# A hybrid decoder block in split fp32: norms of the mixers ended by GpSimd, an earlier weight load and gelu table, square adds on VectorE, and a later start of the second matrix's left factors

## The chip, the cores and the metric

The kernel runs on one core of one Trainium2 chip. The metric is the device time of one execution in microseconds (us), which is the core's span and about 1.7 us around it. The engines are called by the profile's names: PE (TensorE, matrix multiplication), DVE (VectorE), ACT (ScalarE), POOL (GpSimd) and SP (SyncE, which issues most loads).

## The reference

One decoder block over 2048 positions of 1024 features in fp32:

```
h = rms_norm(x, norm1_g)
proj = h @ w_in                                   # u_a, v_a, val_b, gate_b: 512 columns each
# mixer A, four heads of 128 channels
u = gelu(u_a);  v = layer_norm(gelu(v_a), sgu_ln_g, sgu_ln_b)
a = u * (tril(sgu_w[head]) @ v + sgu_b[head])     # over the positions within chunks of 128
# mixer B, four groups of 128 channels
g = val_b * sigmoid(gate_b)
c = depthwise_conv1d(g, conv_w, causal, width 31) + conv_b
c = silu(layer_norm(c, per group of 128 channels))
x = x + concat([a, c]) @ w_out
x = x + relu(rms_norm(x, norm2_g) @ w_ff1)**2 @ w_ff2      # 1024 -> 4096 -> 1024
return rms_norm(x, final_g)
```

## The kernel before

**Arithmetic.** Every fp32 operand of a large product is split into a high part, which a cast on ACT rounds, and a low part, which is the difference, made mostly by POOL (`w_lo`, `h_lo`, `fo_lo`, `w1o`, `w2p`) and now and then by DVE. A product is three matmuls of 128x512 (high x high, low x high, high x low; `mm3`).

**Stages.** The 2048 positions are four blocks of 512. For each block `stage_v` makes the 512 columns of `v_a` (tile `pvv`, four weight tiles of 512 KB, each two slices of 128 features), applies gelu (`gv`) and takes mean and variance on DVE (`vmv`), and then makes `u` (`pu`, gelu at L582). Between them stands the normalisation of `gv` at L585, after which `gate` multiplies it with the masked matrix `wt` (`sgu`). `stage_g` makes gate and value columns (`pg`, `pv`) and starts the convolution: 31 taps on DVE, run in the background (`conv_chain`, `acc<-g,vec,acc`). A finished convolution goes through `conv_tail`: transpose on PE (`ct`), statistics on DVE (`mv`), normalise on ACT (L304, `c<-ct,nb,rs`), transpose back (`cb`), silu (L313, `part<-cb,vec`). `stage_o` is the output projection (`po`).

**A norm's end.** Both norms (`centre` for `gv`, `conv_tail` for `c`) need a scale `rs` = (variance + eps)^-0.5 and a bias `nb` = -mean x rs, 4 values for each partition. DVE makes `ve` = variance + eps, POOL raises it to the power -0.5, DVE multiplies -mean by the result, and ACT normalises with both. In `conv_tail` each `yield` puts the rest off until the clock that the program keeps for PE or DVE has reached the time given.

**The start.** The first four weight tiles come through `load_w`, in order, on SP's queue. `norm1` is a generator whose first step loads two tiles `xin` of the input for the row norm; behind it SP issues `wt` and `cbias`. ACT applies a gelu for the first time at L549.

**The MLP** multiplies matrices in 2x2 blocks with seven products in place of eight (`ORDER`). Its left factors are sums of weight quarters, split in two parts (`w1o`, `w2p`), made during other work and sent to device memory (`w_d`). Its right factors are sums of activations (`fraw`, split into `fo_hi` and `fo_lo`). `down_chunk(pair, n, after)` does step n of the second matrix for a pair of blocks: 28 groups of six matmuls into `py`, each added by DVE to the residual (`x<-py,x`). Between groups `beside` lets other generators run; how many left factors of the second matrix it makes is set by `pace["w2"]`, an amount added at each call. In the last step of a pair (n == 7) every finished `x` is squared on ACT and added up (`square_add`), eight for each block, and a sum over features on PE (`ssum`) gives the final norm.

**What sets the order.** Inside `tc.manual_schedule()` (the output projection, the first matrix, the last step) instructions run in the order in which the code issues them. Everywhere else, the mixers and 15 of the 16 `down_chunk`s among it, a scheduler with a timeline of its own orders each engine's instructions, so an edit in one place also shifts others near it. Each engine then runs its own list in order.

Of the kernel before, what the change touches and what calls it, by code (L numbers as in the profile page):

```python
# [12 lines left out]
AF = mybir.ActivationFunctionType  # L13
ALU = mybir.AluOpType

P = 128
# [20 lines left out]
LAG = 3.0  # L37
# [45 lines left out]
def hybrid_block_kernel(  # L83
# [68 lines left out]
    def tiny(name, n=4):  # L152
        return small.tile([P, n], F32, tag=f"{name}{n}", name=name)
# [83 lines left out]
    nc.vector.memset(ones, 1.0)  # L237
    nhalf = const.tile([P, 1], F32, name="nhalf")
    nc.vector.memset(nhalf, -0.5)
    idle = t2.tile([P, 1024], BF16, tag="tmp", name="idle")[:, :512]  # L240
    nc.vector.memset(idle, 1.0)
    first_bank = tp_tile("first")
# [13 lines left out]

    def centre(mv, rs):

        rsqrt(rs, mv[:, :, 1], 1.0)
        nb = tiny("nb")  # L260
        dve.scalar_tensor_tensor(nb, mv[:, :, 0], -1.0, rs, op0=ALU.mult, op1=ALU.mult)
        return nb


# [18 lines left out]
    def conv_tail(j, c, dst):  # L283

        pt = tp_tile("ct")
        st = small.tile([P, 4, 6], F32, tag="st", name="st")
        mv = small.tile([P, 4, 2], F32, tag="mv", name="mv")
        rs, ve = tiny("rs"), tiny("ve")
        for i in range(4):
            pe4.transpose(pt[:, i * P:(i + 1) * P], c[:, i * P:(i + 1) * P], ident)  # L290
        yield pe.time + 1.0
        for i in range(4):
            dve.bn_stats(st[:, i, :], pt[:, i * P:(i + 1) * P])
        for i in range(4):
            dve.bn_aggr(mv[:, i, :], st[:, i, :])
        dve.tensor_scalar(ve, mv[:, :, 1], 1.0, EPS, op0=ALU.mult, op1=ALU.add)
        yield dve.time + LAG
        gps.tensor_tensor(rs, ve, nhalf.to_broadcast([P, 4]), op=ALU.pow)
        yield pe.time + 1.0
        nb = tiny("nb")  # L300
        dve.scalar_tensor_tensor(nb, mv[:, :, 0], -1.0, rs, op0=ALU.mult, op1=ALU.mult)
        yield dve.time + LAG
        for i in range(4):
            nc.scalar.activation(  # L304
                c[:, i * P:(i + 1) * P], pt[:, i * P:(i + 1) * P], AF.Identity,
                scale=rs[:, i:i + 1], bias=nb[:, i:i + 1])
        yield pe.time + LAG
        pb = tp_tile("cb")
        for i in range(4):
            pe4.transpose(pb[:, i * P:(i + 1) * P], c[:, i * P:(i + 1) * P], ident)  # L310
        yield pe.time + 1.0
        y = dst.place(4 + j, "y")
        nc.scalar.activation(y, pb, AF.Silu, scale=v(V_CG, j), bias=v(V_CBE, j))  # L313
        dst.done(4 + j)
        yield None
# [160 lines left out]
            load_resid(b, kp)  # L476
            yield

    def square_add(acc, src, last=False):

        sq = tmp("sq")[:, :src.shape[1]]
        nc.scalar.activation(sq, src, AF.Square)
        if not acc or last:
            acc.append(sq)
        else:
            gps.tensor_tensor(acc[0], acc[0], sq, op=ALU.add)

    def feature_sums(acc, n, pc=None):

# [197 lines left out]
        nc.sync.dma_start(xk[kp], xt[0, kp].rearrange("p a t -> p (a t)"))  # L687
    r0 = tiny("r1")
    stats = norm1(0, r0)
    next(stats)  # L690
    nc.sync.dma_start(wt, sgu_wt.rearrange("h s t -> s h t"))
    nc.sync.dma_start(cbias, sgu_b.unsqueeze(0).to_broadcast([P, 4, P]))
# [546 lines left out]
    def down_chunk(pair, n, after):  # L1239
# [4 lines left out]
        for i, j in STEPS:  # L1244
# [17 lines left out]
            if n == 7 and LAST[a, t] == i:  # L1262
                done[t] += 1
                if final:
                    sq = tmp("sq")
                    nc.scalar.activation(sq, x, AF.Square)
                    acc = accs[t]
                    if not acc or done[t] > (7 if t else 6):
                        acc.append(sq)
                    else:  # L1270
                        later(1, lambda acc=acc, sq=sq: gps.tensor_tensor(
                            acc[0], acc[0], sq, op=ALU.add))
                    if t == 0 and k_of(done[0]):
                        gained(dn["x"][2], k_of(done[0]))
                else:
                    square_add(accs[t], x)
                if done[t] == 8:
                    if not final:
                        queue.append(finish(2 * pair + t, accs[t]))
                    elif t:  # L1280
                        queue.append(finish_third(3, accs[t]))
                    else:
                        while due:
                            put_off()
                        while queue:
                            if next(queue[0], 0) == 0:
                                queue.pop(0)
                        ends.append(finish_last(2, accs[t], w2[4][0][:, 0, :P], ops[4][0][:, :512]))
# [29 lines left out]
        while due:  # L1318
            beat()
    reopen_banks(mid, "d", mm=8)  # L1320
    pace["w2"] = W2_PACE[3]

    def after_down(pair):
        def after(n, i):
            next(gens, 0)
            if pair == 0 and 2 <= n < 5 and i == 6:
                next(gens)
            if n == 7 and pair == 0:
                for k in range(8):
                    if k * 7 // 8 == DOWN.index(i):  # L1330
                        load_x1(2 + k % 2, k // 2)
        return after
# [57 lines left out]
```

## Time and profile before

| | us |
|---|---|
| median of three runs | 1831.97 (1828.97 to 1837.33) |
| the profiled execution | 1831.89 |
| its span | 1830.2 |
| mean granted clock of PE | 0.997 |
| PE busy | 1809.3 |
| DVE busy | 1330.8 |
| POOL busy | 1233.3 |
| ACT busy | 758.6 |

The busy times are sums over the whole span. The list of waits gives for each pair of waiting and releasing line the total, the number of times and the longest; a row of a timeline gives the start, the time taken, the engine, the line in the code, `out<-in` by the program's names and, in brackets, how long the engine was idle before and what ended that. Lines are those of the kernel before. The three mixers' blocks without output projection run up to about 330 us, the first matrix from about 450 us, and the second from about 1265 us.

### The profile page before, as it was taken

What the parts mean: (1) busy time and instruction counts of PE and PEld (TensorE: products, weight loads), DVE (VectorE), ACT (ScalarE), POOL (GpSimd) and SP (SyncE); (2) the same over time, 40 slices, a digit from 0 to 9 for tenths busy, and PEclk for the clock granted to TensorE, in tenths of its full rate; (3) what the DMA queues carried; (4) which work ended last, traced back from release to release, by engine and by line L of the source; (5) the groups of instructions that cost most, each with busy time, mean ns of one, the idle gap of its engine ahead of it and who ended that gap; (6) DMA issues with size and microseconds to landing.
All of it is one profiled execution on the core that took longest, in us unless ns stands there. A gap on an engine that the chain in (4) does not pass through costs nothing. (4 is left out here: it accounts for less than half of the span.)

```text
span 1830.2 us, 23249 instructions
## 1 busy us (share of the span) xinstructions
PE 1809.3 (99%) x8080; PEld 1488.5 (81%) x8080; DVE 1330.8 (73%) x1825; ACT 758.6 (41%) x1172; POOL 1233.3 (67%) x775
## 2 busy tenths in 40 slices
PE   9999999999999999999999999999999999999998
PEld 6888878888888888888888888888788888888886
DVE  5699997997998985632567787676866568665655
ACT  6345565454445445455354545432322231212112
POOL 4575975883766666699878989776945465444434
PEclk9999999999999999999999999999999999999999
DMA  8342655432645456685557778998987679767652
GB/s 327 112 164 91 229 178 213 184 125 83 220 150 189 161 195 202 215 293 204 208 184 266 270 258 298 355 408 335 412 326 248 252 272 327 299 238 256 254 191 93
DMA packets 131686, 424.74 MB, mean 232 GB/s; under 512 B 14576, under 2 KB 15216, under 8 KB 131568
## 3 DMA queue, kind: packets, MB, share of 16 engines
q1 hardware_dynamic: 96000, 329.12, 50.5%
q10 hardware_dynamic: 35568, 94.13, 13.2%
q8 instruction: 64, 1.05, 0.2%
q14 instruction: 54, 0.44, 0.1%
HBM read 302.60 MB, written 120.59 MB: 231 GB/s over the span
## 5 line engine op out<-in xcount | busy, mean ns | idle before, releaser
L78 PE MATMUL py<-fo_hi,w2o 128*128 128x512 f32 x1792 | 555.9, 391 | 0.8 <-DVE x L78 0.8
L78 POOL TENSOR_TENSOR fo_lo<-fraw,fo_hi 128x1024 fp32r<-128x1024 f32 x111 | 274.4, 2481 | 252.9 <-ACT fo_hi L160 210.7
L78 DVE TENSOR_TENSOR x<-py,x 128x512 f32<-128x512 f32 x448 | 300.9, 687 | 185.8 <-PE py L78 185.4
L78 PEld LDWEIGHTS py<-fo_hi,w2o 128*128 128x128 f32 x1792 | 337.1, 188 | 72.0 <-DVE x L78 1.2
L78 PE MATMUL py<-hop,w1o 128*128 128x512 f32 x1536 | 363.8, 390 | 0.5 <-ACT c L982 0.4
L78 PE MATMUL py<-fo_lo,w2o 128*128 128x512 f32 x896 | 349.7, 390 | 0.9 <-POOL fo_lo L78 0.8
L78 PEld LDWEIGHTS py<-hop,w1o 128*128 128x128 f32 x1536 | 287.6, 188 | 62.4 <-issue 1.4
L78 DVE SCALAR_TENSOR_TENSOR acc<-g,vec,acc 128x512 f32<-128x512 f32 x464 | 322.9, 746 | 1.2
L160 ACT CAST fo_hi<-fraw 128x1024 fp32r<-128x1024 f32 x112 | 117.0, 1052 | 413.7 <-PE py L78 218.0
L78 POOL TENSOR_TENSOR w_lo<-raw,w_hi 128x1024 fp32r<-128x1024 f32 (+1 forms) x94 | 224.1, 2392 | 53.9 <-ACT w_hi L160 39.6
L78 POOL TENSOR_TENSOR w1o<-wraw,w1o 128x512 fp32r<-128x512 f32 x120 | 172.0, 1438 | 55.6 <-ACT w1o L810 43.4
L78 PEld LDWEIGHTS py<-fo_lo,w2o 128*128 128x128 f32 x896 | 168.6, 188 | 37.9 <-POOL fo_lo L78 2.6
L78 PE MATMUL pz<-hop,w1o 128*128 128x512 f32 x768 | 183.8, 390 | 0.0
L78 POOL TENSOR_TENSOR w1o<-ws,w1o 128x512 fp32r<-128x512 f32 x90 | 128.7, 1433 | 66.4 <-ACT w1o L810 62.6
L78 PEld LDWEIGHTS pz<-hop,w1o 128*128 128x128 f32 x768 | 143.8, 188 | 29.8
L78 DVE TENSOR_TENSOR fraw<-fraw 128x1024 f32<-128x1024 f32 x64 | 93.1, 1455 | 13.3 <-POOL fo_lo L78 13.2
L993 ACT ACTIVATE c<-c 128x512 f32<-128x512 f32 x128 | 80.8, 631 | 52.5 <-DVE c L78 52.0
L78 PE MATMUL po<-m_hi,w_hi 128*128 128x512 f32 x256 | 101.1, 395 | 0.0
L78 PE MATMUL po<-m_hi,w_lo 128*128 128x512 f32 x256 | 99.8, 390 | 0.6 <-POOL w_lo L78 0.6
L78 PE MATMUL po<-m_lo,w_hi 128*128 128x512 f32 x256 | 99.7, 389 | 0.0
L78 DVE TENSOR_TENSOR px<-px,c 128x512 f32<-128x512 f32 x32 | 22.3, 698 | 100.9 <-PE px L78 67.8
L78 POOL TENSOR_TENSOR w2p<-wraw,w2p 128x512 fp32r<-128x512 f32 x64 | 93.5, 1463 | 2.6 <-ACT w2p L810 2.6
(155 smaller groups left out, 2947.9 us busy)
## 6 DMA issues: line engine op xcount, KB each, us to landing
w2o<-w_d SPq DMA_DIRECT2D x224, 512.0 KB, 6.0
w_d<-w2p ACTq DMA_DIRECT2D x112, 512.0 KB, 5.4
wraw<-in_w SPq DMA_DIRECT2D x92, 512.0 KB, 4.7
f_d<-c ACTq DMA_DIRECT2D x128, 256.0 KB, 4.1
fraw<-f_d SPq DMA_DIRECT2D x64, 512.0 KB, 6.8
raw<-in_w_ct SPq DMA_DIRECT2D x48, 512.0 KB, 5.0
raw<-in_w_o SPq DMA_DIRECT2D x32, 512.0 KB, 5.4
w1o<-w_d SPq DMA_DIRECT2D x28, 512.0 KB, 5.5
```

What stands on the lines that cost most here:

```text
L78: return op(out, *args, **kwargs)
L160: nc.scalar.copy(hi, src)
L993: later(1, lambda: nc.scalar.activation(c, c, AF.Square))
```

## The change

There are five edits.

1. ACT's first instruction is a gelu on four values (`tiny("table")`), whose result nobody reads.
2. The third weight tile is loaded (`load_w(3)`) before the first step of `norm1`.
3. In `centre` and `conv_tail` DVE makes -mean before the power, and POOL multiplies it by `rs` right after the power in the code. `conv_tail` has one `yield` less.
4. In the last step of the first pair of blocks the fifth to eighth square of each block is added by DVE instead of POOL.
5. `pace["w2"]` is raised to 0.7 not before the second matrix's first step but after its third product (i == 6).

```diff
     nhalf = const.tile([P, 1], F32, name="nhalf")
     nc.vector.memset(nhalf, -0.5)
+    nc.scalar.activation(tiny("table"), nhalf.to_broadcast([P, 4]), AF.Gelu)
...
     def centre(mv, rs):
 
+        nb = tiny("nb")
+        dve.tensor_scalar(nb, mv[:, :, 0], -1.0, None, op0=ALU.mult)
         rsqrt(rs, mv[:, :, 1], 1.0)
-        nb = tiny("nb")
-        dve.scalar_tensor_tensor(nb, mv[:, :, 0], -1.0, rs, op0=ALU.mult, op1=ALU.mult)
+        gps.tensor_tensor(nb, nb, rs, op=ALU.mult)
         return nb
...
         for i in range(4):
             dve.bn_aggr(mv[:, i, :], st[:, i, :])
+        nb = tiny("nb")
+        dve.tensor_scalar(nb, mv[:, :, 0], -1.0, None, op0=ALU.mult)
         dve.tensor_scalar(ve, mv[:, :, 1], 1.0, EPS, op0=ALU.mult, op1=ALU.add)
         yield dve.time + LAG
         gps.tensor_tensor(rs, ve, nhalf.to_broadcast([P, 4]), op=ALU.pow)
+        gps.tensor_tensor(nb, nb, rs, op=ALU.mult)
         yield pe.time + 1.0
-        nb = tiny("nb")
-        dve.scalar_tensor_tensor(nb, mv[:, :, 0], -1.0, rs, op0=ALU.mult, op1=ALU.mult)
-        yield dve.time + LAG
...
-    def square_add(acc, src, last=False):
+    def square_add(acc, src, last=False, e=gps):
...
-            gps.tensor_tensor(acc[0], acc[0], sq, op=ALU.add)
+            e.tensor_tensor(acc[0], acc[0], sq, op=ALU.add)
...
     stats = norm1(0, r0)
+    load_w(3)
     next(stats)
...
-                    square_add(accs[t], x)
+                    square_add(accs[t], x, e=dve if done[t] > 4 else gps)
...
-    pace["w2"] = W2_PACE[3]
 
     def after_down(pair):
         def after(n, i):
+            if pair == 0 and n == 0 and i == 6:
+                pace["w2"] = W2_PACE[3]
```

**SP at the start.** The queue of loads before (`raw` is a weight tile, `xk` the transposed input, `xin` the input for the norm):

```order
L206 DMA raw<-in_w_v 128x1024
L687 DMA xk<-in_xt 128x1024 x3
L411 DMA xin<-in_x 128x1024 x2
L691 DMA wt<-in_sgu_wt 128x4x128
L692 DMA cbias<-in_sgu_b 128x512
L206 DMA raw<-in_w_v 128x1024 x2
L206 DMA raw<-in_w_ct 128x1024
```

and after:

```order
L206 DMA raw<-in_w_v 128x1024
L689 DMA xk<-in_xt 128x1024 x3
L206 DMA raw<-in_w_v 128x1024
L413 DMA xin<-in_x 128x1024 x2
L694 DMA wt<-in_sgu_wt 128x4x128
L695 DMA cbias<-in_sgu_b 128x512
L206 DMA raw<-in_w_v 128x1024
L206 DMA raw<-in_w_ct 128x1024
```

The third weight tile (`raw`) stands ahead of `xin`, `wt` and `cbias`; behind them nothing has moved.

**ACT and POOL in the third block.** ACT before, from the normalise between the third and the fourth gelu (`gv<-pvv`) to the gating's normalise (`gv<-gv,nb,rs`); `c<-ct,nb,rs` is a convolution's normalise, `part<-cb,vec` its silu, `w_hi` a cast of a weight tile:

```order
L304 ACTIVATE c<-ct,nb,rs 128x128 x4
L549 ACTIVATE gv<-pvv 128x512
L160 CAST w1o<-wraw 128x512
L160 CAST w_hi<-raw 128x1024
L582 ACTIVATE u<-pu 128x512
L160 CAST w1o<-wraw 128x512
L160 CAST w_hi<-raw 128x1024
L160 CAST w1o<-ws 128x512
L582 ACTIVATE u<-pu 128x512
L160 CAST w_hi<-raw 128x1024
L160 CAST w1o<-wraw 128x512
L585 ACTIVATE gv<-gv,nb,rs 128x512 x4
```

and after, from the fourth gelu on:

```order
L551 ACTIVATE gv<-pvv 128x512
L160 CAST w_hi<-raw 128x1024
L160 CAST w1o<-wraw 128x512
L160 CAST w_hi<-raw 128x1024
L584 ACTIVATE u<-pu 128x512
L160 CAST w1o<-wraw 128x512
L160 CAST w_hi<-raw 128x1024
```

and on to the gating's normalise:

```order
L160 CAST w_hi<-raw 128x1024
L160 CAST w1o<-wraw 128x512
L306 ACTIVATE c<-ct,nb,rs 128x128 x4
L584 ACTIVATE u<-pu 128x512
L160 CAST w_hi<-raw 128x1024
L315 ACT_TABLE_LOAD
L315 ACTIVATE part<-cb,vec 128x512
L160 CAST w_hi<-raw 128x1024
L584 ACT_TABLE_LOAD
L584 ACTIVATE u<-pu 128x512
L160 CAST m_hi<-part 128x512 x2
L587 ACTIVATE gv<-gv,nb,rs 128x512 x4
```

The convolution's normalise that stood ahead of the fourth gelu now stands behind it, behind four casts of weight tiles and behind the second `u`, and the gating's normalise, which stood behind the second `u`, stands behind the fourth.

POOL at the same place, before, from the gating's power (`rs<-ve,nhalf`) on:

```order
L78 TENSOR_TENSOR rs<-ve,nhalf 128x4
L78 TENSOR_TENSOR w_lo<-raw,w_hi 128x1024
L78 TENSOR_TENSOR w1o<-ws,w1o 128x512
L527 COPY g<-halo 128x30
L78 TENSOR_TENSOR w_lo<-raw,w_hi 128x1024
L78 TENSOR_TENSOR w1o<-wraw,w1o 128x512
L78 TENSOR_TENSOR w_lo<-raw,w_hi 128x1024 x2
```

and after, with the powers and the products (`nb<-nb,rs`) of this block's norms:

```order
L78 TENSOR_TENSOR rs<-ve,nhalf 128x4
L78 TENSOR_TENSOR w1o<-wraw,w1o 128x512
L78 TENSOR_TENSOR w_lo<-raw,w_hi 128x1024
L78 TENSOR_TENSOR w1o<-wraw,w1o 128x512
L78 TENSOR_TENSOR rs<-ve,nhalf 128x4
L78 TENSOR_TENSOR nb<-nb,rs 128x4
L78 TENSOR_TENSOR w_lo<-raw,w_hi 128x1024
L78 TENSOR_TENSOR w1o<-ws,w1o 128x512
L529 COPY g<-halo 128x30
L78 TENSOR_TENSOR w_lo<-raw,w_hi 128x1024
L78 TENSOR_TENSOR w1o<-wraw,w1o 128x512
L78 TENSOR_TENSOR nb<-nb,rs 128x4
```

Of the two products the first has three other instructions and a second power between itself and its power, and the second stands behind the first and five others.

**DVE at the first pair's last step.** Before there are the additions to the residual (`x<-py,x`) and the sums for right factors (`fraw`) only:

```order
L78 TENSOR_TENSOR x_10285<-py,x_10285 128x512
L78 TENSOR_TENSOR x_10160<-py,x_10160 128x512
L78 TENSOR_TENSOR fraw<-fraw 128x1024
L78 TENSOR_TENSOR x_10205<-py,x_10205 128x512
L78 TENSOR_TENSOR fraw<-fraw 128x1024
L78 TENSOR_TENSOR x_10247<-py,x_10247 128x512
L78 TENSOR_TENSOR x_10285<-py,x_10285 128x512
L78 TENSOR_TENSOR x_10160<-py,x_10160 128x512
L78 TENSOR_TENSOR x_10205<-py,x_10205 128x512
```

After, at the same place, the square adds (`sq<-sq`) stand between:

```order
L78 TENSOR_TENSOR sq<-sq 128x512
L78 TENSOR_TENSOR x_10307<-py,x_10307 128x512
L78 TENSOR_TENSOR sq<-sq 128x512
L78 TENSOR_TENSOR x_10180<-py,x_10180 128x512
L78 TENSOR_TENSOR sq<-sq 128x512
L78 TENSOR_TENSOR fraw<-fraw 128x1024
L78 TENSOR_TENSOR x_10225<-py,x_10225 128x512
L78 TENSOR_TENSOR sq<-sq 128x512
L78 TENSOR_TENSOR x_10267<-py,x_10267 128x512
```

Four adds have come in among four additions to the residual, and a right factor's sum stands right behind the third.

## The prediction

> **What bounds the kernel now.** I read the busy shares first, then the list of TensorE's waits, then the granted clock around the longest of them, and then the chain behind each.
>
> ```profile
> PE 1809.3 (99%) x8080; PEld 1488.5 (81%) x8080; DVE 1330.8 (73%) x1825; ACT 758.6 (41%) x1172; POOL 1233.3 (67%) x775
> ```
>
> TensorE (PE) is busy 99% of the span, and the change leaves its matmuls as they are in kind and number. One starts every 1809.3/8080 = 0.224 us. So nothing is to be had but TensorE's idle time and its time at a lower clock.
>
> ```profile
> PE sgu L78 <- ACT gv L585: 3.0, 1, 3.0
> ...
> PE pvv L78 <- ACT h_hi L707: 1.5, 1, 1.5
> PE pu L78 <- ACT w_hi L160: 1.0, 1, 1.0
> PE ssum L78 <- POOL sq L78: 1.0, 1, 1.0
> PE pu L78 <- ACT gv L549: 1.0, 1, 1.0
> PE py L78 <- POOL fo_lo L78: 0.8, 2, 0.6
> PE py L78 <- DVE x L78: 0.8, 1, 0.8
> PE cb L78 <- ACT c L304: 0.6, 1, 0.6
> ```
>
> Columns: us in total, times, the longest. These rows sum to 9.7 us, and each is one that the change reaches for. Each wait costs some 0.2 us more than its row says, because a matmul's listed 0.39 us overlaps the next one's start.
>
> ```profile
> 17.00:22.00 5.00, 3.52 (x20) 2.89 (x19) 3.42 (x7) 4.49 (x7) 0.00 (x0) 1.00 1.03 410
> 30.00:35.00 5.00, 4.02 (x18) 2.96 (x18) 4.03 (x10) 4.99 (x7) 0.80 (x2) 1.00 1.02 408
> 244.00:252.00 8.00, 6.55 (x24) 4.97 (x25) 7.96 (x13) 7.59 (x9) 3.85 (x3) 0.79 0.56 200
> 1503.00:1508.00 5.00, 5.00 (x18) 4.02 (x18) 3.23 (x4) 0.00 (x0) 5.00 (x4) 0.66 0.78 274
> ```
>
> The third number from the right is the granted clock. Behind the two early waits it is 1.00. Behind the 3.0 us wait it is 0.79 over 8 us, a loss of 8 x 0.21 = 1.7 us, and behind the ssum wait 0.66 over 5 us, again 1.7 us.
>
> **The start (third tile's load, first gelu).**
>
> ```profile
> 5.05 1.17 SPq L411 DMA_DIRECT2D xin<-in_x  x2
> ...
> 8.22 1.60 SPq L206 DMA_DIRECT2D raw<-in_w_v  x2
> ```
>
> ```profile
> 13.33 1.06 ACT L419 ACTIVATE junk<-xin 128x1024 bf16<-128x1024 f32 x1 [2.49 <-DMA xin<-in_x]
> ...
> 17.51 1.04 ACT L160 CAST w_hi<-raw 128x1024 fp32r<-128x1024 f32 x1 [1.65 <-DMA raw<-in_w_v]
> ...
> 29.85 1.28 ACT L549 ACT_TABLE_LOAD   x1 [3.90 <-PE pvv L78]
> ```
>
> ```profile
> 30.51 0.39 PE L78 MATMUL pvv<-w_hi,h_lo 128*128 128x512 f32 x1
> 31.88 0.50 PE L78 MATMUL pu<-h_hi,w_hi 128*128 128x512 f32 x1 [0.98 <-ACT gv L549]
> ```
>
> The third weight tile is issued behind two norm tiles, the mask and the biases, and ScalarE (ACT) gets it at 17.51. Put ahead of them it lands about where the first norm tile does, 13.3: 4.2 us sooner against a wait of 1.5. The norm's tiles come one 512 KB transfer later (0.5 MB at the 410 GB/s shown is 1.3 us); all behind it in the queue lands as before, and the norm is wanted only by the gelus at 31. Gain 1.5 + 0.2 = 1.7. The gelu table now loads while ScalarE waits for its first data, and the 1.28 us load at 29.85 goes, under which TensorE waited: 31.88 - 30.51 - 0.22 = 1.15. What could be late next is the first norm scale, which I take to be hidden. **A = 2.9.**
>
> The Trainium skill, "ScalarE: Activation LUTs", section "What ACT_TABLE_LOAD costs", adds a drain of about 1.4 us to such a load. The trace has the next gelu at 31.14, right behind the load, so the row gives no sign of it and the estimate by that page (2.7 us off ScalarE) would not change TensorE's 1.15.
>
> **The mixers' norms.** Before, VectorE (DVE) makes the variance term `ve`, GpSimd (POOL) the power `rs`, VectorE again the bias `nb`, ScalarE normalises. After, VectorE makes -mean and `ve` together, and GpSimd multiplies.
>
> ```profile
> 236.93 0.16 DVE L78 TENSOR_SCALAR ve<-vmv 128x4 f32<-128x4 f32 x1
> ...
> 243.64 0.63 DVE L78 SCALAR_TENSOR_TENSOR nb<-vmv,rs 128x4 f32<-128x4 f32 x1
> ```
>
> ```profile
> 237.16 1.01 POOL L78 TENSOR_TENSOR rs<-ve,nhalf 128x4 f32<-128x4 f32 x1 [1.27 <-DVE ve L78]
> ```
>
> ```profile
> 228.42 1.51 ACT L304 ACTIVATE c<-ct,nb,rs 128x128 f32<-128x128 f32 x4 [4.18 <-DVE nb L78]
> ...
> 244.36 2.23 ACT L585 ACTIVATE gv<-gv,nb,rs 128x512 f32<-128x512 f32 x3 [6.11 <-DVE nb L78]
> ```
>
> ```profile
> 231.92 0.50 PE L78 MATMUL pu<-h_hi,w_hi 128*128 128x512 f32 x1 [1.01 <-ACT w_hi L160]
> ...
> 241.80 0.39 PE L78 MATMUL pu<-h_hi,w_hi 128*128 128x512 f32 x1
> 245.23 0.49 PE L78 MATMUL sgu<-wt,gv 128*128 128x128 f32 x2 [3.04 <-ACT gv L585]
> ```
>
> In the third block the power is there at 238.17, but VectorE reaches `nb` at 243.64, behind convolution taps: 5.5 us lost, and TensorE pays 3.04. Earlier there, ScalarE stands 4.18 us for another `nb`, with a weight cast behind it for which TensorE waits 1.01.
>
> The product's price on GpSimd is not in the trace. Bounds:
>
> ```profile
> L531 POOL COPY halo<-g 128x30 f32<-128x30 f32 x12 | 2.6, 216 | 20.7 <-DVE g L78 16.3 <-DMA hf<-in_xt 4.3
> ```
>
> ```profile
> L78 POOL TENSOR_TENSOR rs<-ve,nhalf x20: 996/1010/1378, 37.1 to 689.7; 128x4 f32<-128x4 f32 x20
> ...
> L78 DVE SCALAR_TENSOR_TENSOR nb<-mv,rs x16: 150/846/5953, 133.7 to 694.3; 128x4 f32<-128x4 f32 x16
> ```
>
> ```profile
> 100.00:400.00 300.00, 295.07 (x1365) 243.20 (x1364) 281.25 (x482) 156.47 (x229) 223.02 (x152) 0.99 0.47 166
> ```
>
> At least 0.22 (a small copy), at most 1.01 (the power on as many elements); it cannot be negative, being work added. I take 0.25, nearest the copy, since a plain product has no power to form: 20 x 0.25 = 5 us, at most 20, on an engine idle 300 - 223 = 77 us in 100 to 400. The cover is that idle time; without it the next weight's low part would be 0.25 to 1.0 late per norm.
>
> The new order decides more than the price. ScalarE now runs the third block's four gelus and the weight cast ahead of the convolution's normalise, so the 1.01 wait goes. The gating's normalise comes after the fourth u, and by the order its matmuls stand 44 later on TensorE, 9.9 us: ready for them at 242.0 + 9.9 = 251.9, less A and the 1.2 gained, 247.7. Against that, GpSimd's product stands behind two weight low parts and two left factors; by the power's end at 238.2, two at 2.4, two at 1.3, a copy of 0.2 and 0.25 it is ready at 246.1, and ScalarE's first result 0.8 later, at 246.9. It arrives 0.8 us ahead, or 5 ahead if GpSimd gains the 4.1 too. So the waits go: 1.01 + 3.04 + 0.4 (two restarts) and the clock's 1.7. **B = 6.15.** The late convolution in the fourth block (0.6, its `nb` the one that took 5953 ns) has the product right behind the power: **C = 0.8.**
>
> The Trainium skill, "TensorE: Matmul & The Clock Gate", section "What's actually happening", has the clock halved after an idle window of about 3.4 us. The stop of 3.04 us with 0.79 behind it fits that; the ssum wait is only 1.0 us and has 0.66 behind it, so there the row goes beyond the rule. By the rule alone, ending the ssum wait would return nothing of that clock, and the sum below would be about 0.85 smaller.
>
> **First steps of the second matrix.**
>
> ```profile
> 1262.86 0.62 ACT L810 CAST w2p<-ws 128x512 fp32r<-128x512 f32 x1 [18.87 <-PE py L78]
> ...
> 1265.72 1.05 ACT L160 CAST fo_hi<-fraw 128x1024 fp32r<-128x1024 f32 x1 [2.25 <-DMA w2o<-w_d]
> ```
>
> At 0.7 for each of four calls, some 2.8 left factors are not made in the first step. ScalarE's cast of the right factors stood behind one that had waited 18.87 us for a slot; now it comes 1265.72 - 1262.86 = 2.9 us sooner, and GpSimd's low part with it. That covers the two fo_lo waits (0.8) and, partly, VectorE's 0.8: 1.6 + three restarts of 0.2 = 2.2, of which I take **E = 2.0**. The factors are made up afterwards, in steps where TensorE waits for none.
>
> **Square adds on VectorE.**
>
> ```profile
> 1502.29 1.05 PE L78 MATMUL ssum<-ones,sq 128*128 128x1 f32 x8 [1.01 <-POOL sq L78]
> ```
>
> ```profile
> 1498.44 3.80 POOL L78 TENSOR_TENSOR sq<-sq 128x512 f32<-128x512 f32 x3
> ```
>
> ```profile
> L78 DVE TENSOR_TENSOR ws<-wraw,ws x44: 674/1770/2873, 534.2 to 1296.9; 128x512 f32<-128x512 f32 x44
> ```
>
> ```profile
> L78 DVE TENSOR_TENSOR x<-py,x 128x512 f32<-128x512 f32 x448 | 300.9, 687 | 185.8 <-PE py L78 185.4
> ```
>
> Eight adds move; each takes 0.67 to 2.87 us on VectorE (same shape, both inputs in SBUF). At 0.67 they fit between evictions of 0.69 and the whole 1.0 + 0.2 + 1.7 = 2.9 comes back; at 2.87 the four ahead of the sum take 11.5 us, and a new wait of a few us stands here. I take the median, 1.77, where the last add ends about as late as GpSimd's did, and credit half: **F = 1.45.**
>
> The row says: an add with two SBUF inputs spreads from 674 to 2873 ns, an eviction from PSUM stays near 687. The Trainium skill, "SBUF — State Buffer", section "Who interferes with whom", names the reason: a VectorE instruction with two SBUF inputs contends with a GpSimd instruction that reads SBUF. The trace agrees; by that rule F would be nothing or less.
>
> **Sum.** 2.9 + 6.15 + 0.8 + 2.0 + 1.45 = 13.3. From this I take 1.3, three waits of the size of the smallest listed (0.4 to 0.6), for an order that the scheduler has reshuffled through 400 us. 1831.9 - 12.0 = 1819.9 us, from the profiled execution's 1831.89; the median of the runs, 1831.97, is 0.1 above that.
>
> **Rivals.**
> - The norm chain stays late. For: the products stand 6 to 10 us behind their powers in three chains, and 0.8 us of margin is little. Against: GpSimd gains time at the start too. Then B is nothing: 1820 + 6.15 = 1826.
> - VectorE's adds are blocked (2.87 each): F turns from +1.45 to a wait of some 3, 1820 + 4.5 = 1824.5. For: GpSimd runs without a break there (5.00 of 5.00 us). Against: the pair that starts first keeps its speed, and 674 occurs.
> - The start gives nothing, since the 410 GB/s are spent either way and another load is late: 1820 + 2.9 = 1823.
> - Slower. In order, ScalarE stands at a normalise for the product, and the weight casts behind it starve TensorE, now that products queue behind GpSimd's long subtracts. The three chains hold 24 us of such work (6.0, 7.8 and 10.4); if all reached TensorE, 1820 + 24 = 1844. It decides from 12 + 9.2 = 21 us lost. Against: of the 4.18 + 6.11 us that ScalarE stood for `nb` in the third block, 4.05 reached TensorE.
>
> **How the numbers follow.** A measurement of this kernel tells about 0.5% (9.2 us) from no change. Chances: forecast 0.55 (own range 1814 to 1823), late chain 0.20, blocked adds 0.12, start without gain 0.07, slower 0.06. Below 1822.8 lies nearly all of the first and a little of the third and fourth: faster 0.57, same 0.37, slower 0.06. The range runs from 1813 (all 13.3, the whole of F and a little more) to 1830 (late chain and blocked adds together), leaving out the slow case and the tails.
>
> **What would show it.** After: no row sgu <- gv and no pvv <- h_hi in the waits; a table load before 5 us and none near 30; nb on GpSimd at 0.2 to 0.4 us; the clock 1.00 around 245; the adds on VectorE at 0.67 or at 1.8 and above. I am wrong if sgu, pu or po wait several us for a normalise, or the clock still falls near 1500.

## The result and the profile after

| | before | changed |
|---|---|---|
| median | 1831.23 us (6 runs, 1828.97 to 1837.33) | 1819.53 us (6 runs, 1818.07 to 1820.28) |
| span of the profiled execution | 1830.2 us | 1817.8 us |

The ratio of the times is 0.9928 (95% interval 0.9914 to 0.9942). The forecast was 1820.

TensorE's waits after, from the list of waits (us in total, times, longest), complete:

```profile
PE first L245 <- DVE idle L242: 1.7, 1, 1.7
PE py L78 <- DVE x L78: 1.0, 1, 1.0
PE pu L78 <- ACT gv L551: 0.7, 1, 0.7
PE po L78 <- POOL w_lo L78: 0.6, 1, 0.6
PE py L78 <- ACT c L985: 0.5, 1, 0.5
PE sgu L78 <- DVE u L78: 0.4, 1, 0.4
PE rbc L78 <- DVE dg L78: 0.2, 1, 0.2
```

None of the eight waits that the prediction listed stands at its place any more. Three new ones have come: for x near 1508, for a gelu in the third block, and for `u` at a later sgu, 2.1 us together. The clock around the places where it had dropped, from the table by windows (third number from the right):

```profile
240.00:252.00 12.00, 12.00 (x64) 10.23 (x63) 11.68 (x18) 11.39 (x16) 10.65 (x8) 1.00 0.43 148
...
1490.00:1500.00 10.00, 9.83 (x42) 7.47 (x41) 7.38 (x6) 3.35 (x5) 8.79 (x5) 1.00 0.69 237
1500.00:1512.00 12.00, 11.03 (x49) 8.78 (x48) 12.00 (x21) 1.06 (x1) 1.82 (x1) 1.00 0.77 268
```

The third block's gating on GpSimd, ScalarE and TensorE, from the timelines:

```profile
231.83 1.01 POOL L78 TENSOR_TENSOR rs<-ve,nhalf 128x4 f32<-128x4 f32 x1
232.80 0.20 POOL L78 TENSOR_TENSOR nb<-nb,rs 128x4 f32<-128x4 f32 x1
...
240.32 0.20 POOL L78 TENSOR_TENSOR nb<-nb,rs 128x4 f32<-128x4 f32 x1
```

```profile
245.11 2.93 ACT L587 ACTIVATE gv<-gv,nb,rs 128x512 f32<-128x512 f32 x4
```

```profile
248.98 1.95 PE L78 MATMUL sgu<-wt,gv 128*128 128x128 f32 x16
```

The power ends at 232.8. The product at 232.80 is the convolution's; the gating's comes 7.5 us behind its own power, at 240.32. Nobody waits for it: ScalarE gets to the normalise at 245.11 without a bracket, the first of the four is done 0.8 later, and TensorE begins sgu 3 us after that, without a wait.

What one instruction took, from the views of the tiles (minimum, median, maximum in ns):

```profile
L78 POOL TENSOR_TENSOR nb<-nb,rs x20: 188/198/802, 35.1 to 680.8; 128x4 f32<-128x4 f32 x20
```

```profile
L78 DVE TENSOR_TENSOR sq<-sq x8: 676/694/2301, 1477.8 to 1501.3; 128x512 f32<-128x512 f32 x8
```

The product costs 0.2 us. Of the eight adds five take 0.68 to 0.69 and three 2.26 to 2.30.

**Where the 12.3 us of span went.** I took the start of the same matmul (the n-th into the same tile) in both traces and compared the lead over the kernel before at the ends of six stretches. The last columns do the same for the experiments below, against the same trace of before (us, minus is a gain):

| stretch | changed | n1 both norms | n4 conv norm | n3 gating norm | n2 yield | s1 start | s2 load | s3 pace | s4 adds | c4 no norms |
|---|---|---|---|---|---|---|---|---|---|---|
| start, to the second matmul of pu | -2.25 | 0.22 | 0.54 | 1.20 | 0.36 | -2.61 | -2.14 | 0.09 | 0.56 | -2.27 |
| third block, from its pvv to the first po | -5.57 | -5.61 | -7.55 | -0.02 | 1.13 | -0.10 | -0.96 | 5.44 | -0.24 | 2.26 |
| fourth block's pvv and pu | -1.11 | -1.15 | -1.11 | -1.09 | -1.97 | -1.15 | -1.12 | -1.12 | -1.11 | -1.15 |
| second matrix, first steps | -3.20 | 0.24 | 0.24 | -0.22 | 0.26 | -0.43 | -0.42 | -3.20 | 0.02 | -3.07 |
| first pair's last step | -1.04 | 0.01 | 0.01 | -1.59 | 0.03 | -1.48 | 0.02 | 0.01 | -1.09 | -1.09 |
| end | 1.08 | 0 | 0.94 | 0.95 | 0.94 | 0.03 | 0.95 | 0 | 0 | 0.04 |

The rest lies between these stretches and is under 1 us in each trace. The table is read by rows. An edit did something where its column differs from the columns without it, not where it differs from zero: zero is one execution of before. So the fourth block's 1.1 us is in every column, with the edit and without it. The third block's row ends at the first matmul of `po`, which in n4 stands six matmuls earlier in TensorE's order than in the others of the table; up to the fourth block's first `pvv` the gains are 5.5 (changed), 5.6 (n1) and 6.8 (n4).

### The profile page after: what moved, and what is told of

It is laid out like the page before. It is cut to its first block, busy times and chain, and to the rows that moved or that the text cites. A ratio compares the mean times of both kernels' runs of the same rounds, so it can differ in the third digit from the quotient of the medians.

```text
span 1817.8 us, 23247 instructions
## 1 busy us (share of the span) xinstructions
PE 1805.2 (99%) x8080; PEld 1488.0 (82%) x8080; DVE 1318.6 (73%) x1832; ACT 754.6 (42%) x1170; POOL 1232.4 (68%) x788
## 3 DMA queue, kind: packets, MB, share of 16 engines
q10 hardware_dynamic: 35568, 94.13, 13.2%
## 4 chain that ended last, share of the span: by engine, by line
PE 92%; DVE 6%; issue 1%; POOL 1%; DMA 0%; ACT 0%; POOLq 0%; SPq 0%; DVEq 0%; ACTq 0%
PE py L78 51%; PE pz L78 9%; PE po L78 9%; PE px L78 5%; PE pv L78 4%; PE pg L78 4%; PE pu L78 4%; PE pvv L78 4%; DVE acc L78 3%; PE sgu L78 1%; PE rbc L78 0%; PE ssum L78 0%; DMA raw<-in_w_o 0%; PE cb L78 0%; PE ct L78 0%
## 5 line engine op out<-in xcount | busy, mean ns | idle before, releaser
L78 POOL TENSOR_TENSOR fo_lo<-fraw,fo_hi 128x1024 fp32r<-128x1024 f32 x112 | 283.0, 2535 | 260.6 <-ACT fo_hi L160 231.1
```

The source lines that it names most:

```text
L78: return op(out, *args, **kwargs)
```

## The experiments

Two theories stood at first. T: VectorE's second trip in the norms (product `nb` behind the power) is what ScalarE and then TensorE wait for. O: the scheduler's changed order did it, whichever engine multiplies.

**n1: the norms' edit alone.**

```diff
     def centre(mv, rs):
+        nb = tiny("nb")
+        dve.tensor_scalar(nb, mv[:, :, 0], -1.0, None, op0=ALU.mult)
         rsqrt(rs, mv[:, :, 1], 1.0)
-        nb = tiny("nb")
-        dve.scalar_tensor_tensor(nb, mv[:, :, 0], -1.0, rs, op0=ALU.mult, op1=ALU.mult)
+        gps.tensor_tensor(nb, nb, rs, op=ALU.mult)
...
+        nb = tiny("nb")                                       # conv_tail
+        dve.tensor_scalar(nb, mv[:, :, 0], -1.0, None, op0=ALU.mult)
         dve.tensor_scalar(ve, mv[:, :, 1], 1.0, EPS, op0=ALU.mult, op1=ALU.add)
         yield dve.time + LAG
         gps.tensor_tensor(rs, ve, nhalf.to_broadcast([P, 4]), op=ALU.pow)
+        gps.tensor_tensor(nb, nb, rs, op=ALU.mult)
         yield pe.time + 1.0
-        nb = tiny("nb")
-        dve.scalar_tensor_tensor(nb, mv[:, :, 0], -1.0, rs, op0=ALU.mult, op1=ALU.mult)
-        yield dve.time + LAG
```

> The kernel before with the norms' edit alone (both functions, product on GpSimd). Theory T (the second trip to VectorE was what ScalarE and TensorE waited for): the third block's waits of 1.0 and 3.0 us and the clock of 0.79 go (5.5 us as the changed kernel showed it), and so does the fourth block's (1.1 us); about 6.6 us less than before, 1825, and nothing beyond the mixers. Rival O (the other edits shifted the scheduler's order, and that did it): under 2 us.

Measured: 1825.15 us, ratio 0.9965 (0.9948 to 0.9981). The third block gains 5.6, the waits of 1.0 and 3.0 us are gone. This is T's number; O is out for the other edits, but not for the edit's own reordering.

**n2: one yield less, product on VectorE.**

```diff
+        nb = tiny("nb")                                       # conv_tail
         dve.tensor_scalar(ve, mv[:, :, 1], 1.0, EPS, op0=ALU.mult, op1=ALU.add)
         yield dve.time + LAG
         gps.tensor_tensor(rs, ve, nhalf.to_broadcast([P, 4]), op=ALU.pow)
+        dve.scalar_tensor_tensor(nb, mv[:, :, 0], -1.0, rs, op0=ALU.mult, op1=ALU.mult)
         yield pe.time + 1.0
-        nb = tiny("nb")
-        dve.scalar_tensor_tensor(nb, mv[:, :, 0], -1.0, rs, op0=ALU.mult, op1=ALU.mult)
-        yield dve.time + LAG
```

> The kernel before with one yield less in the convolution's norm, its product still on VectorE, right behind the power in the code. In its order the convolution's normalise stands behind the third block's fourth gelu, as in the changed kernel, but the gating's product is still on VectorE and its matmuls stand as early as before. Theory T: the wait of 1.0 us goes, the one of 3.0 with its clock stays: 1.2 us less, 1830. Rival O (issuing in fewer steps does it, whichever engine multiplies): about 6 us less, 1825.

Measured: 1832.68 us, ratio 1.0007 (0.9994 to 1.0020). Both numbers were wrong (1830 and 1825): the waits of 1.0 and 3.0 us are gone, and one of 4.8 us has come earlier, at 208 among the third block's `pvv`, on a convolution's norm:

```profile
PE cb L78 <- ACT c L303: 4.8, 1, 4.8
```

```profile
L78 DVE SCALAR_TENSOR_TENSOR nb<-mv,rs x16: 130/1066/7804, 134.1 to 690.2; 128x4 f32<-128x4 f32 x16
```

The instruction behind it is a product of four elements a partition that took 7.8 us on VectorE. Issuing in fewer steps is no gain while that product is there.

**n3: the gating's norm alone on GpSimd.**

```diff
     def centre(mv, rs):
+        nb = tiny("nb")
+        dve.tensor_scalar(nb, mv[:, :, 0], -1.0, None, op0=ALU.mult)
         rsqrt(rs, mv[:, :, 1], 1.0)
-        nb = tiny("nb")
-        dve.scalar_tensor_tensor(nb, mv[:, :, 0], -1.0, rs, op0=ALU.mult, op1=ALU.mult)
+        gps.tensor_tensor(nb, nb, rs, op=ALU.mult)
```

> The kernel before with the gating's norm alone on GpSimd (centre). Its gating matmuls stand 23 later in the third block than before. Theory T: the wait of 3.0 us and its clock's 1.7 go, the other waits (1.0 and the fourth block's 0.6) stay: 4.5 to 5 us less, 1826.5. Rival O: with the convolution's norm as before the order is about as before, and less than 2 us goes.

Measured: 1831.86 us, ratio 1.0009 (0.9999 to 1.0018). T had 1826.5 and failed. The wait of 3.0 us is gone as T said, but two of 2.5 us stand in the third block, at 212 and 233, both through the convolution's norm, whose product VectorE still makes. Ahead of the first that product was held for 8.04 us; ahead of the second the next one took only 0.14 us, at 227.72, but stood behind sixteen taps in VectorE's list:

```profile
PE pu L78 <- ACT w_hi L160: 2.5, 1, 2.5
PE cb L78 <- ACT c L305: 2.5, 1, 2.5
```

```profile
202.45 8.04 DVE L78 SCALAR_TENSOR_TENSOR nb<-mv,rs 128x4 f32<-128x4 f32 x1
```

**n4: the convolution's norm alone on GpSimd.**

```diff
+        nb = tiny("nb")                                       # conv_tail only
+        dve.tensor_scalar(nb, mv[:, :, 0], -1.0, None, op0=ALU.mult)
         dve.tensor_scalar(ve, mv[:, :, 1], 1.0, EPS, op0=ALU.mult, op1=ALU.add)
         yield dve.time + LAG
         gps.tensor_tensor(rs, ve, nhalf.to_broadcast([P, 4]), op=ALU.pow)
+        gps.tensor_tensor(nb, nb, rs, op=ALU.mult)
         yield pe.time + 1.0
-        nb = tiny("nb")
-        dve.scalar_tensor_tensor(nb, mv[:, :, 0], -1.0, rs, op0=ALU.mult, op1=ALU.mult)
-        yield dve.time + LAG
```

> The kernel before with the convolution's norm alone on GpSimd (conv_tail). Theory T: the wait of 1.0 us and the fourth block's 0.6 go (2 us), the gating's product still comes from VectorE, so a wait of 1 to 3 us at sgu stays, perhaps with the lower clock: 2 to 4 us less, 1829. Rival O: as much as with both, 6 us less.

Measured: 1824.62 us, ratio 0.9968 (0.9948 to 0.9989): as much as with both. T, which wanted a wait at sgu, failed here too. The gating's product is still on VectorE, 2.6 us behind its power, and costs nothing. Timelines of n4 in the third block, VectorE, GpSimd, ScalarE and TensorE:

```profile
229.48 0.16 DVE L78 TENSOR_SCALAR ve<-vmv 128x4 f32<-128x4 f32 x1
236.31 1.20 DVE L78 SCALAR_TENSOR_TENSOR nb<-vmv,rs 128x4 f32<-128x4 f32 x1
```

```profile
232.72 1.01 POOL L78 TENSOR_TENSOR rs<-ve,nhalf 128x4 f32<-128x4 f32 x1
```

```profile
237.61 2.94 ACT L585 ACTIVATE gv<-gv,nb,rs 128x512 f32<-128x512 f32 x4 [1.75 <-DVE nb L78]
```

```profile
244.04 1.05 PE L78 MATMUL sgu<-wt,gv 128*128 128x128 f32 x8
```

Before, the gating's variance term began at 236.93; here at 229.48. Before, ScalarE stood 4.18 us at a convolution's normalise with the fourth gelu behind it, so the statistics, the term, the power and the product of the gating were all late. What that normalise waited for, from the timelines of before, VectorE and GpSimd:

```profile
210.01 6.27 DVE L78 TENSOR_SCALAR ve<-mv 128x4 f32<-128x4 f32 x1
216.20 10.62 DVE L78 SCALAR_TENSOR_TENSOR acc<-g,vec,acc 128x512 f32<-128x512 f32 x16
...
227.98 0.40 DVE L78 SCALAR_TENSOR_TENSOR nb<-mv,rs 128x4 f32<-128x4 f32 x1
```

```profile
216.36 1.02 POOL L78 TENSOR_TENSOR rs<-ve,nhalf 128x4 f32<-128x4 f32 x1
```

The power was done at 217.38, and VectorE came to the product 10.6 us later, behind sixteen taps; ahead of the power the variance term had taken 6.27 us. So the 3.0 us at sgu were the end of a chain of two trips, the convolution's and the gating's. n3 takes out the second, and the wait goes there too, though its gating matmuls also stand 23 later.

What holds of T is this. In before, n2 and n3 the convolution's product is on VectorE, and TensorE's longest wait in the third block, 2.5 to 4.8 us, is for a norm or for what stands behind one. In n1, n4 and the changed kernel it is on GpSimd, and no wait there is for a norm (at most 0.7 us is for a gelu). n2 and n4 issue in equally many steps, and their main difference is the engine of that product (the scheduler also orders some taps differently): 1832.68 against 1824.62 us. So its engine is shown to be the cause of the gain. It is not shown to be the only way to end the two waits of before, since n2 has neither of them.

**s1 and s2: the start.** s1 has the first gelu and the earlier load, s2 the load alone.

```diff
+    nc.scalar.activation(tiny("table"), nhalf.to_broadcast([P, 4]), AF.Gelu)    # s1 only
...
     stats = norm1(0, r0)
+    load_w(3)
     next(stats)
```

> The kernel before with the first gelu and the third tile's earlier load alone. By the prediction 2.9 us less; by the changed kernel's trace 1.7 at the third tile and 1.0 at the gelu, less 0.4 that its first matmul began later. If that 0.4 belongs to the gelu ahead of the first cast, it is here too (2.3 less in all); if it is only when the first load lands, 2.7 to 3. Rival (410 GB/s are spent either way): the wait only moves, 1 us or less.

> The kernel before with the third tile's earlier load alone: the wait of 1.5 us for it goes (1.7 less), the one of 1.0 behind the gelu table stays. Rival: the row norm's tiles, 1.3 us later, hold up the first gelus, and the second wait grows by what the first saves.

Measured: s1 1829.57 us, ratio 0.9988 (0.9971 to 1.0005); s2 1827.47 us, ratio 0.9974 (0.9961 to 0.9988). The times of s1 spread over almost 10 us and do not tell it from before. By the traces the start gains 2.6 and 2.1, and s2's first matmul began 0.4 later than before's while s1's began 0.1 later, so from there on both gain about 2.6. What was said of s2's second wait was wrong: with the load alone it goes too. Timelines of s2, ScalarE and TensorE:

```profile
26.44 1.28 ACT L549 ACT_TABLE_LOAD   x1 [1.38 <-PE pvv L78]
27.74 1.85 ACT L549 ACTIVATE gv<-pvv,r 128x512 f32<-128x512 f32 x3
29.82 0.69 ACT L549 ACTIVATE gv<-pvv,r 128x512 f32<-128x512 f32 x1 [0.24 <-PE pvv L78]
```

```profile
29.77 0.48 PE L78 MATMUL pu<-h_hi,w_hi 128*128 128x512 f32 x1
```

The table is still loaded here, for 1.28 us, but from 26.44, under TensorE's last `pvv` matmuls, and the last gelu waits for TensorE. The first gelu at the kernel's start is then worth nothing that these runs can tell; TensorE, VectorE and GpSimd have the same list of instructions in s1 and s2. The 0.4 by which the changed kernel's first matmul began later belongs to neither edit: n2 and n3, which have before's start, also began 0.4 later. In s2, n3 and the changed kernel the twelve matmuls of the tile `idle` (`first`) ahead of it took 5.30 us, in before 4.46.

**s3: the pace alone.**

```diff
-    pace["w2"] = W2_PACE[3]
...
         def after(n, i):
+            if pair == 0 and n == 0 and i == 6:
+                pace["w2"] = W2_PACE[3]
```

> The kernel before with the later pace alone. The prediction took 2.0 of the 2.2 to 2.8 us that TensorE loses in the second matrix's first steps; the changed kernel lost none there and was 3.0 us shorter over that stretch. If the left factors' casts ahead of the right factors' were the cause: 2.5 to 3 us less. If VectorE's sums or the loads were: under 1 us, with waits for x or w2o in place of those for fo_lo.

Measured: 1827.92 us, ratio 0.9970 (0.9952 to 0.9989). The first steps gain 3.20 us, with no wait for fo_lo or x left there, and so do all kernels with the edit (3.1 to 3.2; c1 to c3, which are not in the table, too), against a gain of 0.4 to a loss of 0.3 in those without. The left factors that are no longer made in these steps are shown to be the cause. Which part of making them it is, the casts, the low parts or the loads, was not separated.

The profile of s3 also lost 5.4 us in the third block, where the lists of instructions of TensorE, VectorE, ScalarE and GpSimd are those of before. The clock behind the stop of 3.0 us at sgu was lower than in before:

```profile
244.00:252.00 8.00, 6.69 (x22) 5.67 (x23) 7.96 (x13) 7.51 (x9) 3.93 (x3) 0.57 0.61 203
```

That is 0.57 against 0.79, but from 241 to 262 only 0.4 us were lost. The other 5.0 were lost between 262 and 277, at a convolution's product on VectorE. Timelines of before, VectorE, and of s3, VectorE and TensorE:

```profile
269.95 1.81 DVE L78 SCALAR_TENSOR_TENSOR nb<-mv,rs 128x4 f32<-128x4 f32 x1
```

```profile
270.05 6.73 DVE L78 SCALAR_TENSOR_TENSOR nb<-mv,rs 128x4 f32<-128x4 f32 x1
```

```profile
278.37 0.69 PE L78 MATMUL ct<-ident,c 128*128 128x128 f32 x4 [3.24 <-ACT c L304]
```

GpSimd ran the same instructions beside both. In before the product ended with the first of them, here with the fifth. So how long such a product is held differs between executions of the same list, and it can cost TensorE several microseconds.

**s4: the square adds alone.**

```diff
-                    square_add(accs[t], x)
+                    square_add(accs[t], x, e=dve if done[t] > 4 else gps)
```

> The kernel before with the eight square adds on VectorE alone. The ssum wait of 1.0 us and the 0.66 clock behind it go (2.9 us), and a wait of TensorE for VectorE's additions to the residual comes near 1520, 1.0 to 1.3 us, since the adds, the sums for the right factors and the scaling of the first block stand ahead of them: 1.5 us less in all. If the lower clock belongs to the eight narrow matmuls of ssum rather than to the wait, it stays, and all of it is within 0.5 us of before. If GpSimd blocks the adds, they take 1.8 to 2.9 each, and the time is 1 to 3 us longer.

Measured: 1833.17 us, ratio 1.0006 (0.9985 to 1.0026): the time does not tell. The trace has five adds at 0.68 to 0.69 us and three at 2.25 to 2.30, no wait at ssum, the clock at 1.00 over 1500 to 1512, and a new wait for x of 1.0 us. The last step gains 1.09. But s1 gains 1.48 and n3 1.59 there without the edit. In s1 the wait at ssum stands, and the clock does not drop:

```profile
PE ssum L78 <- POOL sq L78: 1.0, 1, 1.0
```

```profile
1498.50:1504.00 5.50, 5.50 (x28) 4.62 (x28) 3.81 (x5) 0.16 (x1) 5.50 (x4) 1.00 0.76 268
```

Whether the clock drops behind this wait differs from one execution to the next: of the eleven traces that have the wait, it drops in eight and not in s1, n3 and c3. In the three with the whole edit (the changed kernel, s4 and c4) the wait is gone and the clock stays at 1.00, at the price of about 1.3 us of new wait. That the edit shortens the kernel on average is not shown.

**c1: the changed kernel, adds on VectorE for the block t == 0 alone.**

```diff
-                    square_add(accs[t], x, e=dve if done[t] > 4 else gps)
+                    square_add(accs[t], x, e=dve if done[t] > 4 and t == 0 else gps)
```

> The changed kernel with the square adds on VectorE for the first block alone. Theory: TensorE's wait of 1.0 us for x near 1508 comes from VectorE's queue, in which four adds of the second block stand ahead of the additions to the residual; with those back on GpSimd the wait goes, 1.0 to 1.3 us less than the changed kernel (1818.3). Rival: the eight scaled writes of the first block and the product for the broadcast (2.9 us) hold VectorE as long; the wait stays and the time is the same within 0.5 us.

Measured: 1820.41 us, ratio 0.9926 (0.9904 to 0.9948). I had the blocks the wrong way round: the sum that comes first in the code's order belongs to t == 1. So the wait at ssum is back and the one for x is gone, and with both the last step has no gain left (it loses 0.1). TensorE's wait for x near 1508 does not come with the second sum's adds alone. The version that keeps just the first sum's was not run. The intervals of c1 and of the changed kernel overlap, so the times do not tell which is better.

**c2: c1 with the gating's product back on VectorE.**

```diff
     def centre(mv, rs):                                       # against c1
-        nb = tiny("nb")
-        dve.tensor_scalar(nb, mv[:, :, 0], -1.0, None, op0=ALU.mult)
         rsqrt(rs, mv[:, :, 1], 1.0)
-        gps.tensor_tensor(nb, nb, rs, op=ALU.mult)
+        nb = tiny("nb")
+        dve.scalar_tensor_tensor(nb, mv[:, :, 0], -1.0, rs, op0=ALU.mult, op1=ALU.mult)
```

> As the run before it, and with the gating's product back on VectorE (the convolution's norm alone ends on GpSimd). In the single runs the convolution's norm alone took 2 us more off the third block than both together. If that holds with the earlier start: 1816 to 1817, no wait at sgu, and none of 0.7 for the gelu in the third block. Rival T: the gating's trip back to VectorE costs the sgu wait again, 3 us and a lower clock: 1822 or more.

Measured: 1818.15 us, ratio 0.9916 (0.9893 to 0.9938). The third block gains 7.5, 1.9 more than in the changed kernel, as n4 did, and there is no wait for a norm in it. Up to the fourth block's first `pvv` it is 1.1 more (6.6 against 5.5), since here too the first `po` stands six matmuls earlier. Its median lies 1.4 us below the changed kernel's and 2.3 below c1's, the intervals overlap; that it beats the changed kernel is likely by the traces and not shown by the times.

**c3: c2 with the whole end of the convolution's norm on GpSimd.**

```diff
-        nb = tiny("nb")                                       # conv_tail, against c2
-        dve.tensor_scalar(nb, mv[:, :, 0], -1.0, None, op0=ALU.mult)
-        dve.tensor_scalar(ve, mv[:, :, 1], 1.0, EPS, op0=ALU.mult, op1=ALU.add)
         yield dve.time + LAG
+        gps.tensor_scalar(ve, mv[:, :, 1], 1.0, EPS, op0=ALU.mult, op1=ALU.add)
         gps.tensor_tensor(rs, ve, nhalf.to_broadcast([P, 4]), op=ALU.pow)
+        nb = tiny("nb")
+        gps.tensor_scalar(nb, mv[:, :, 0], -1.0, None, op0=ALU.mult)
         gps.tensor_tensor(nb, nb, rs, op=ALU.mult)
```

> As the run before it, and with all of the convolution's norm's ending on GpSimd: its variance term and -mean as well, so that VectorE has no instruction of four values there. Theory: VectorE's instructions of four values are held (up to 5.4 us) while GpSimd runs its subtracts without a break; without them the gelus' statistics come up to 5 us sooner, TensorE waits nowhere in the mixers for a norm, and the time is that of the run before it or up to 1 us less. Rival: two more instructions on GpSimd per norm (32 x 0.2 us) make the weights' low parts late, and a wait of TensorE for w_lo of 0.5 us or more comes.

Measured: 1820.03 us, ratio 0.9932 (0.9906 to 0.9957). No further gain: the third block gains 6.2, less than c2's 7.5, with a wait of 0.7 for a gelu. No wait for w_lo came beside the 0.6 that all have. Moving VectorE's instructions ahead of the power is then worth nothing that can be seen here. Whether their hold cost something in the kernel before, where the variance term took 6.27 us, no run separates.

**c4: the changed kernel without the norms' edit.**

```diff
-        gps.tensor_tensor(nb, nb, rs, op=ALU.mult)            # both norms as in the kernel before
+        dve.scalar_tensor_tensor(nb, mv[:, :, 0], -1.0, rs, op0=ALU.mult, op1=ALU.mult)
```

> The changed kernel without the norms' edit. If the edits add up: the changed kernel's time and 6.5 us, 1826, with the waits of 1.0 and 3.0 us in the third block and its clock of 0.8. If the other edits made the norms' gain smaller or larger (the scheduler's order moves as a whole): outside 1824 to 1828.

Measured: 1824.59 us, ratio 0.9958 (0.9944 to 0.9973); against 1819.53 the norms' edit is worth 5.1 by the medians and 6.5 by the spans (1824.3 and 1817.8). The edits add up within that, but the waits are not those expected: the 1.0 and 3.0 us are gone and one of 6.8 has come. Timelines of VectorE, GpSimd, ScalarE and TensorE:

```profile
203.47 10.45 DVE L78 SCALAR_TENSOR_TENSOR nb<-mv,rs 128x4 f32<-128x4 f32 x1
```

```profile
200.67 1.00 POOL L78 TENSOR_TENSOR rs<-ve,nhalf 128x4 f32<-128x4 f32 x1
201.65 2.38 POOL L78 TENSOR_TENSOR w_lo<-raw,w_hi 128x1024 fp32r<-128x1024 f32 x1
...
211.56 2.34 POOL L78 TENSOR_TENSOR w_lo<-raw,w_hi 128x1024 fp32r<-128x1024 f32 x1
```

```profile
213.95 1.50 ACT L305 ACTIVATE c<-ct,nb,rs 128x128 f32<-128x128 f32 x4 [10.82 <-DVE nb L78]
```

```profile
215.51 1.12 PE L78 MATMUL cb<-ident,c 128*128 128x128 f32 x4 [6.81 <-ACT c L305]
```

A product of four elements a partition began at 203.47 and ended at 213.92, 0.02 us after the last of nine instructions that GpSimd ran without a gap (201.65 to 213.90). ScalarE waited for it, and TensorE for ScalarE. Neither the start nor the order of the instructions explains it. Up to about 1190 us the lists of TensorE, VectorE, ScalarE and GpSimd are the same in c4 and s1, and there the same product took a third of the time, with the waits of 1.0 and 3.0 us later. VectorE of s1:

```profile
203.13 3.10 DVE L78 SCALAR_TENSOR_TENSOR nb<-mv,rs 128x4 f32<-128x4 f32 x1
```

In s1 it ended with the third of the nine instructions. So the waits in one trace of a kernel with this product on VectorE are one draw of several; that the edit gains is carried by the times of all runs.

## Why the prediction was right, point by point

- **The time**: 1819.5 against 1820. The closeness is partly luck. The sum was made against one execution. The five stretches gain 13.2 against its 13.3, because E and the fourth block make up for the 1.6 by which A, B and F fell short, and in place of the 1.3 taken off 1.08 was lost at the end, where nothing was changed. Neither the fourth block's 1.1 nor the end's 1.08 is the change's.
- **A, start, 2.9**: measured 2.25 against before's trace. In the traces without the edit the start came 0.1 to 1.2 later than in that one (mean of n1 to n4, s3 and s4: 0.5), so the size holds: 2.25 + 0.5 = 2.75. The step "the 1.28 us load at 29.85 goes, under which TensorE waited: 1.15" failed as an account: s2 gets it from the weight tile alone, and the first gelu adds nothing.
- **B, third block, 6.15**: 5.6 measured against before's trace; the traces without the edit lie between 1.0 below and 5.4 above that one. The estimate of 0.25 us for the product was near (0.20), and the margin was 3 us, inside the 0.8 to 5 given. What failed is the account of the 3.04 us by VectorE reaching the gating's `nb` at 243.64 "behind convolution taps" alone. n3 shows that moving the gating's product alone gains nothing in all, and n4 that moving the convolution's gains as much as both. I had the two waits as separate; they were one chain, and its first link, too, was a product behind taps. The bracket that says it was among my quoted rows: ScalarE's 4.18 us for `nb`, ahead of the fourth gelu.
- **C, fourth block, 0.8**: the wait at cb is in the execution of before that I read and in none of s1 to s4, which run the same code there. The product that took 5.95 us in before took 1.65 to 1.66 in those four, and the variance term ahead of it 4.23 to 4.24 in place of 0.60. The 1.1 us of the table's third row are no gain of the change.
- **E, first steps, 2.0**: 3.2 measured, mis-sized by 1.2. I credited part of the listed waits; VectorE's wait for x went whole, and the stretch's small stops that the list does not show went with them.
- **F, square adds, 1.45**: 1.04 measured. I took a median of 1.77 us for an add and half of the gain, with the ssum wait half gone. The median was 0.69, the ssum wait and its clock went whole (2.9), and what came back was 1.0 us and its restart at x and smaller stops. Half was right for the wrong reason. s1 and n3 show besides that 1.5 of it comes in some executions without the edit.
- **The allowance of 1.3**: three new waits, 2.1 us, of which the one for x belongs to F.
- **Rivals**: "blocked adds" came in part: three of eight at 2.3 us beside GpSimd's subtracts, too few to make the sum late. By the Trainium skill, "SBUF — State Buffer", section "Who interferes with whom", such adds contend with GpSimd's reads; those three rows agree. Of the other five, which took no longer than an eviction, three found GpSimd idle, one stood beside its power, and one began 0.02 us ahead of a subtract. "Late chain" was right on the product, 7.5 us behind its power, and wrong on what waits for it. "Slower" did not come about, though ScalarE still stood for `nb` as the view of the tile says (us, times):

```profile
  POOL nb L78: 24.4, 10
```

  Before, it was 34.6 us in nine places. TensorE's list of waits has none for a normalise behind these 24.4 us.

## What to carry to other kernels

A wait in the list names the last link: follow the engine that ended it back through its own brackets to the first one before a cost is given to an instruction. A tiny instruction on VectorE between two engines can be the longest link of all, because it stands behind long ones in the list or because GpSimd runs without a break, so keep the end of such a chain on the engine that made its input. And take two or three traces of the kernel before: terms of 1 us that stand in one trace may be missing from the next, and here a wait of 6.8 us was in one of two traces with the same lists.

## What the runs showed of the hardware that was not expected

A VectorE product of 128x4 with both inputs in SBUF took 0.13 us when GpSimd stood still (n2, at 227.79) and up to 5.95 (before), 7.80 (n2), 8.04 (n3) and 10.45 us (c4). The last ended with GpSimd's unbroken run of nine instructions, not with the first of them. Others end with the first: the gating's product of before at 243.64, after 0.63 us, with a subtract that ended at 244.25, while GpSimd went straight on. And the length is not a property of the place: the same product in the same lists took 1.81 (before) and 6.73 us (s3), and 3.10 (s1) and 10.45 us (c4). What decides it, these runs do not show. An instruction that reads a mean only is held as well:

```profile
220.22 5.44 DVE L78 TENSOR_SCALAR nb<-mv 128x4 f32<-128x4 f32 x1
```

That is the changed kernel, and GpSimd's run there ends at 225.6 too. The taps of the convolution, whose accumulator is in PSUM, are not held by the same work of GpSimd, 24 in a row in 17.48 us:

```profile
237.65 17.48 DVE L78 SCALAR_TENSOR_TENSOR acc<-g,vec,acc 128x512 f32<-128x512 f32 x24
```

The Trainium skill, "SBUF — State Buffer", section "Who interferes with whom", says of VectorE's two-port modes that whoever issues first holds the shared ports for the whole instruction and the other blocks. The rows agree that VectorE blocks, and the long ones go further: it stood through several of GpSimd's instructions, not through one.

The clock behind a stop differs between executions of the same code: 0.79 and 0.57 behind the same 3.0 us, and behind the same 1.0 us at ssum 0.66 in before and 1.00 in s1. The end shows it too. Windows over the last narrow matmuls, of before and of the changed kernel:

```profile
1817.00:1822.00 5.00, 4.67 (x24) 3.13 (x23) 4.01 (x9) 0.00 (x0) 1.76 (x2) 1.00 0.87 320
```

```profile
1804.00:1809.00 5.00, 5.00 (x20) 3.25 (x20) 3.35 (x7) 0.00 (x0) 1.36 (x2) 0.68 0.91 348
```

Nothing was changed there, and the changed kernel's profiled execution lost its 1.1 us at that place. What decides it, these runs do not show.
